# State space input weights from tables of powers spread in DRAM instead of 64 transposes, with two additions held back and another order of the last stores

## The chip, the cores and the metric

The kernel runs on one core of one Trainium2 chip. Its engines are TensorE (PE in the profile, with its weight loads as PEld), VectorE (DVE), ScalarE (ACT), GpSimd (POOL) and SyncE (SP, which here only issues DMAs). The metric is the device time in microseconds; the time of a kernel is the median of its runs. One execution is also recorded by the profiler. All durations below come from that execution, and its span runs from the first to the last instruction.

## The reference, cut to what matters

A one-layer encoder over two sequences of 512 tokens with 1024 channels: three branches (a state space branch, differential attention, cross attention to a memory), gated and summed, then a gated feed-forward part and a final RMS norm. All of it is f32. The change touches the state space branch and the end:

```python
lam_bar = jnp.exp(lam * step[:, None])
b_bar = ((lam_bar - 1.0) / lam)[..., None] * b
bu = jnp.einsum('lgh,gph->lgp', u.astype(jnp.complex64), b_bar)
_, xs = lax.associative_scan(_ssm_combine, (a, bu), axis=0)
...
return x + (jax.nn.silu(gate) * up) @ p['w_ffn_out'][l]
...
return _rmsnorm(x, p['norm_final'])
```

There are 32 groups (g) of 16 channels (h) and 64 complex states, in two directions, so that 2 x 64 states fill the 128 partitions.

## The kernel before, in words

Every large product is made on TensorE from a high and a low part of each f32 operand (three products `xh*wh`, `xl*wh`, `xh*wl`, each 128x128 by 512 columns). `weight` (L146) loads a 128x1024 tile of weights by an SP DMA into `wf` (two buffers); `split` casts it to `wh` on ScalarE (L134) and subtracts to get `wl` on VectorE (L135), two buffers each. The order of work is: memory projections (`mem_k`, `mem_v`), norm of the inputs x (`x_norm`, L252 to L254), four tiles of the u projection (weights `w_in[0]` to `w_in[3]`), gate projections with the state space work in between, gelu and its gate product, cross attention, differential attention, merge, output product, feed-forward, final norm.

The state space branch is a generator, `s5_gen`, advanced by `next(s5)` at fixed places of the program:

- the second step, during `mem_k`, computes powers 0 to 8 of `lam_bar` (`pr`, `pi`) and the factor `gr`, `gi` on VectorE in small operations (L1433 to L1544);
- the third, issued on SP behind the load of `w_in[1]`, loads `b` and `c` (L1549 to L1552);
- the fourth, behind the split of `w_in[1]` on ScalarE and VectorE, makes `b_r`, `b_i` (b times the factor), copies the powers turned for the two directions (`qr`, `qi`, `xr_`, `xi_`, L1564 to L1567) and calls `input_weights` for three of the four blocks of eight groups;
- the fifth, after the u projection in the program, makes `output_weights` 0 and 1, loads `u_`, multiplies it by the input weights (L1668), makes the fourth block of input weights and `output_weights` 2 and 3;
- then the scan over 64 chunks of 8 tokens (four VectorE operations each, L1683 to L1686), and the outputs (L1727 to L1729).

`input_weights(o)` multiplies, on VectorE, `b_r` and `b_i` by the powers (six operations of 128x1024, L1590 to L1592). The result has the states on the partitions; the product with u needs (token in chunk, channel) there. So each of its 16 blocks of 128x128 is transposed on TensorE (L1604) into PSUM and copied out by ScalarE (L1605): 64 transposes and 16 copies of 512 columns in all.

Near the end, the feed-forward output product runs in 12 visits of 128 output rows by a seven-product scheme. In the last eight of its 36 pieces the weights' sums are not prepared ahead: `raw_sums` (L452 to L455) makes four of them on GpSimd, ScalarE (L137) and VectorE (L138) split them, and TensorE uses them one piece later. At the end of each visit GpSimd adds four quadrants to y (L1301), in the order c11, c22, c21, c12.

The final norm goes in three column ranges (512, 256, 256). In the last one TensorE spreads the row factors into PSUM (L69), ScalarE copies them to SBUF for GpSimd (L1356), GpSimd scales rows 0 to 2 (L1359) and VectorE rows 3 to 7 (L1364), and SP stores pairs of rows (L1367).

The order of instructions on each engine is set when the kernel is built: a planner takes the ready instruction that stands first in the program, by a simulated timeline; some blocks are told to come after a given instruction of the same engine (`queued()`: after the last weight load on SP; `yielding(...)`: after a split). At run time each engine, and SP's queue, goes in that fixed order and waits where it must.

Of the kernel before, what the change touches and what calls it, by code (L numbers as in the profile page):

```python
# [10 lines left out]
F32 = mybir.dt.float32  # L11
# [61 lines left out]
def encoder(ctx: ExitStack, tc: tile.TileContext, a, out):  # L73
# [375 lines left out]
    def raw_sums(raw):  # L449

        a21, a11, a12, a22 = (raw[:, i] for i in range(4))
        PO.tensor_tensor(out=a22, in0=a21, in1=a22, op=ALU.add)  # L452
        PO.tensor_tensor(out=a21, in0=a11, in1=a21, op=ALU.subtract)
        PO.tensor_tensor(out=a11, in0=a22, in1=a11, op=ALU.subtract)
        PO.tensor_tensor(out=a12, in0=a12, in1=a11, op=ALU.subtract)  # L455
# [770 lines left out]
    n_w, last_7, last_h = 0, None, None  # L1226

    def w_room(n):
        nonlocal n_w
# [3 lines left out]

    def weights7(i, m, p, n):

        nonlocal last_w, last_7, last_h
# [29 lines left out]
    next(coming[0], None)  # L1266
    with queued(), tc.issue_after(last_h.ins):
        nxt = act_pair(2, third=V)
    n_p = 0
    for v, (m, lo_, hi_) in enumerate(VISITS):  # L1270
        ps = [bank() for _ in range(6)] + [aux()]
        for p in range(lo_, hi_):
            if n_p + 3 < len(pieces) and not pieces[n_p + 3][2]:
                next(coming[n_p + 3])
            if n_p + 2 < len(pieces):
                next(coming[n_p + 2])
            for g in coming[n_p + 1 : n_p + 2]:
                for _ in g:
                    pass
            th, tl = pairs[p]  # L1280
            w = made[n_p]
            n_p += 1
            if v < 4 and p == 1:
                with queued():
                    for t in (m, m + 4):
                        nc.sync.dma_start(y[t], x1D[t])
            for p_, (nm, o) in zip(ps, SEVEN):
                wh, wl = w[nm]
                PE.matmul(p_, wh, th[:, o], start=(p == lo_), stop=False)
                PE.matmul(p_, wh, tl[:, o], start=False, stop=False)  # L1290
                PE.matmul(p_, wl, th[:, o], start=False, stop=(p == hi_ - 1))
            if v == 3 and p == 0:
                with queued(), tc.issue_after(last_sum.ins):
                    pair_in()
            if (v, p) in ((10, 7), (10, 8), (11, 7), (11, 8)):
                keep(2)
        ps = iter(ps)
        c11, c12, c21, c22 = quadrants(ps, next(ps), ("nsq", "nsq"))
        for c_, t, s in ((c11, 0, 0), (c22, 4, 1), (c21, 4, 0), (c12, 0, 1)):
            yv = y[m + t][:, s * L : (s + 1) * L]  # L1300
            PO.tensor_tensor(out=yv, in0=yv, in1=c_, op=ALU.add)  # L1301
        if v == 0:
            with tc.issue_after(last_sum.ins):
                pairs.append(quad_split(2, *nxt))
            with tc.issue_after(last_q[1].ins):
                activate(1, gf1, up1)
        elif v == 1:
            with queued(), tc.issue_after(last_sum.ins):
                pair_in()
        if v == 2:  # L1310
            with queued():
                nc.sync.dma_start(aD[KFF - 1], ac)
        if v == 7:
# [36 lines left out]
    def final(ss, c0, n, ready=(), late=()):  # L1350

        cs = slice(c0, c0 + n)
        _, bc = factor(ss, DM, n // P)
        if ready:
            b_ = new_acc()
            S.copy(b_[:, :n], bc[:, :n])  # L1356
        for m in (0, 1, 4, 5, 6, 7, 2, 3) if late else range(KD):
            if m in ready:
                PO.tensor_tensor(out=y[m][:, cs], in0=y[m][:, cs], in1=b_[:, :n], op=ALU.mult)  # L1359
            else:  # L1360
                with ExitStack() as es_:
                    if m in late:
                        es_.enter_context(tc.issue_after(last_add.ins))
                    V.scalar_tensor_tensor(out=y[m][:, cs], in0=y[m][:, cs], scalar=vcol("norm_final", m), in1=bc[:, :n],  # L1364
                                           op0=ALU.mult, op1=ALU.mult)
            if m % 2 == 1:
                nc.sync.dma_start(out[c0 // L, :, m - 1 : m + 1, c0 % L : c0 % L + n], y2[m // 2][:, :, cs])  # L1367
            yield

# [79 lines left out]
def s5_gen(k):  # L1449
# [67 lines left out]
    def cmul(eng, outr, outi, ar, ai, br, bi, t1, t2):  # L1517
# [4 lines left out]
        eng.tensor_tensor(out=t2, in0=ai, in1=br, op=ALU.mult)  # L1522
        eng.tensor_tensor(out=outi, in0=t1, in1=t2, op=ALU.add)

    ta, tb = (pp.tile([P, 512], F32, name=n_) for n_ in ("ta", "tb"))
# [26 lines left out]
    nc.sync.dma_start(cn, a["c_im"])  # L1552
    yield

    V.tensor_scalar_mul(cn, cn, -1.0)
    b_r, b_i = cp.tile([P, G, 16], F32, name="b_r"), cp.tile([P, G, 16], F32, name="b_i")
    bs = [P, G, 16]
    cmul(V, b_r, b_i, br, bi, gr.unsqueeze(2).broadcast_to(bs), gi.unsqueeze(2).broadcast_to(bs),
         ta.rearrange("p (g h) -> p g h", h=16), tb.rearrange("p (g h) -> p g h", h=16))

    qr, qi = cp.tile([P, 8, G], F32, name="qr"), cp.tile([P, 8, G], F32, name="qi")
    xr_, xi_ = cp.tile([P, 8, G], F32, name="xr_"), cp.tile([P, 8, G], F32, name="xi_")
    for (q_, x_, s_) in ((qr, xr_, pr), (qi, xi_, pi)):
        S.copy(q_[0:64], s_[0:64, 7::-1, :])  # L1564
        S.copy(q_[64:128], s_[64:128, 0:8, :])
# [27 lines left out]
        return tiles  # L1593


    def input_weights(o):
        res = []
        for w_ in cprod("it", by_group(b_r, o), by_group(b_i, o), by_token(qr, o), by_token(qi, o), True):
            w_ = w_.rearrange("p g e h -> p (g e h)")
            t_ = slot("wb", [P, 8 * P], name="wb")  # L1600
            for g4 in range(2):
                tr = aux()
                for g in range(4):
                    PE.transpose(tr[:, g * P : (g + 1) * P], w_[:, (4 * g4 + g) * P : (4 * g4 + g + 1) * P], ident)  # L1604
# [57 lines left out]
    for o in range(4):  # L1662
        for ri, w_ in enumerate(wbs[o]):
            for g4 in range(2):
# [110 lines left out]
def layout(i):  # L1775
# [31 lines left out]
    a["log_step"] = dpg(np.broadcast_to(i["s5_log_step"][0][:, :, None], (2, G, 64)))  # L1807
    for nm in ("re", "im"):
        b = i["s5_b_" + nm][0]
        a["b_" + nm] = b.transpose(0, 2, 1, 3).reshape(P, G, 16)  # L1810
        c = i["s5_c_" + nm][0]
        a["c_" + nm] = c.transpose(0, 3, 1, 2).reshape(P, G, 16)
# [21 lines left out]
```

## Time and profile before

| | |
|---|---|
| median of 3 runs | 1589.17 us (1587.68 to 1589.8) |
| the profiled execution | 1588.24 us |
| its span | 1586.5 us |
| mean granted TensorE clock | 0.998 |
| instructions | 21339 |
| TensorE instructions | 7736 matmuls and as many weight loads |
| HBM read, written | 165.16 MB, 71.27 MB |

A row of a group of instructions names line, engine, operation, what is written from what, and the shape; then the count, the busy time and the mean of one. Matmuls overlap in the pipeline, so the start of one to the start of the next is what one costs, and not its duration. In a row of the timeline the first number is the start in us and the second how long the (merged) entry took; idle time before it, and what ended it, stands in brackets.

### The profile page before, as it was taken

To read this page: it belongs to the slowest core of one execution; us is meant where nothing else is said; L and a number is where in the kernel's file an instruction comes from. 1 tells how busy PE (TensorE), PEld (TensorE's weight loads), DVE (VectorE), ACT (ScalarE), POOL (GpSimd) and SP (SyncE) were. 2 spreads that over 40 slices of the span, in tenths; PEclk is the share of its full clock that TensorE was granted. 3 is DMA by queue.
4 is the path that set the end of the run, shared out by engine and by line. 5 is a ranking of instruction groups with operands and counts; after the bars stand their busy time and mean duration, and the time that the engine had idled before them with its cause. 6 is when DMAs were issued, how large, how long until landed. Compare 5 with 4: busy or idle time off the path is not lost. (4 is left out here: it accounts for less than half of the span.)

```text
span 1586.5 us, 21339 instructions
## 1 busy us (share of the span) xinstructions
PE 1573.4 (99%) x7736; PEld 1311.3 (83%) x7736; DVE 1169.2 (74%) x1859; ACT 631.9 (40%) x1115; POOL 550.7 (35%) x434
## 2 busy tenths in 40 slices
PE   9999999999999999999999999999999999999997
PEld 7888888888898779778888888888888888888777
DVE  7978995076774776866545669888888877888864
ACT  7644223265553365563223443333333324222323
POOL 0010000001333320300443355777777553444763
PEclk9999999999999999999999999999999999999999
DMA  9554623676762121135544422323333323885412
GB/s 359 186 170 127 204 94 119 179 266 205 266 223 107 41 100 41 47 127 179 196 143 126 141 86 93 119 101 120 120 128 125 114 85 124 319 315 189 152 56 107
DMA packets 105610, 237.84 MB, mean 150 GB/s; under 512 B 13600, under 2 KB 45344, under 8 KB 105504
## 3 DMA queue, kind: packets, MB, share of 16 engines
q1 hardware_dynamic: 105360, 236.45, 44.4%
q8 instruction: 61, 1.00, 0.3%
q14 instruction: 45, 0.37, 0.1%
q10 hardware_dynamic: 144, 0.02, 0.0%
HBM read 165.16 MB, written 71.27 MB: 149 GB/s over the span
## 5 line engine op out<-in xcount | busy, mean ns | idle before, releaser
L66 PE MATMUL bkmm<-xh,wh 128*128 128x512 f32 x640 | 255.6, 399 | 0.0
L66 PE MATMUL bkmm<-xh,wl 128*128 128x512 f32 x640 | 250.9, 392 | 0.0
L66 PE MATMUL bkmm<-xl,wh 128*128 128x512 f32 x640 | 250.4, 391 | 0.0
L66 PE MATMUL bkmm<-tl,wh 128*128 128x512 f32 (+1 forms) x621 | 241.4, 389 | 0.0
L66 PE MATMUL bkmm<-th,wl 128*128 128x512 f32 (+1 forms) x621 | 241.0, 389 | 0.0
L66 PE MATMUL bkmm<-th,wh 128*128 128x512 f32 (+1 forms) x621 | 240.9, 389 | 0.0
L134 ACT CAST wh<-wf 128x1024 fp32r<-128x1024 f32 (+2 forms) x134 | 117.6, 878 | 265.4 <-PE bkmm L66 190.7
L135 DVE TENSOR_TENSOR wl<-wf,wh 128x1024 fp32r<-128x1024 f32 (+2 forms) x134 | 147.6, 1102 | 61.0 <-ACT wh L134 45.7
L66 PE MATMUL bkmm<-th,w 128*128 128x512 f32 x432 | 140.6, 392 | 2.6 <-ACT w L137 2.1
L66 PEld LDWEIGHTS bkmm<-xh,wh 128*128 128x128 f32 x640 | 120.4, 188 | 26.2 <-issue 3.4
L66 PEld LDWEIGHTS bkmm<-xh,wl 128*128 128x128 f32 x640 | 120.3, 188 | 26.0 <-issue 0.4
L66 PEld LDWEIGHTS bkmm<-xl,wh 128*128 128x128 f32 x640 | 120.5, 188 | 22.3
L66 PEld LDWEIGHTS bkmm<-th,wl 128*128 128x128 f32 x621 | 116.6, 188 | 24.0
L66 PEld LDWEIGHTS bkmm<-th,wh 128*128 128x128 f32 x621 | 116.6, 188 | 23.9
L66 PEld LDWEIGHTS bkmm<-tl,wh 128*128 128x128 f32 x621 | 116.7, 188 | 23.8
L1175 POOL TENSOR_TENSOR up<-up,acc 128x512 f32<-128x512 f32 x44 | 83.7, 1919 | 90.7 <-DVE up L1112 87.0
L452 POOL TENSOR_TENSOR raw<-raw 128x128 f32<-128x128 f32 x28 | 14.7, 523 | 287.4 <-DVE nb L543 230.7
L66 PEld LDWEIGHTS bkmm<-th,w 128*128 128x128 f32 x432 | 81.0, 188 | 22.0 <-ACT w L137 3.0
L792 POOL TENSOR_TENSOR mg<-mg,gl 128x1024 f32<-128x1024 f32 x16 | 43.8, 2740 | 136.8 <-DVE gl L788 132.1
L66 PE MATMUL bkmm<-tl,w 128*128 128x512 f32 x216 | 84.2, 390 | 0.0
L134 ACT CAST wh<-ws 128x1024 fp32r<-128x1024 f32 x44 | 46.3, 1053 | 91.5 <-PE bkmm L66 49.8
L66 PE MATMUL bkmm<-yh,wh 128*128 128x512 f32 x192 | 76.3, 397 | 0.0
(661 smaller groups left out, 3534.6 us busy)
## 6 DMA issues: line engine op xcount, KB each, us to landing
wf<-in_w_in SPq DMA_DIRECT2D x40, 512.0 KB, 3.9
wD<-hl SPq DMA_DIRECT2D x28, 512.0 KB, 2.9
w<-wD SPq DMA_DIRECT2D x28, 512.0 KB, 5.2
gD<-gt SPq DMA_DIRECT2D x24, 512.0 KB, 2.8
gl<-gD SPq DMA_DIRECT2D x24, 512.0 KB, 3.7
wf<-in_w_fg SPq DMA_DIRECT2D x22, 512.0 KB, 3.6
wf<-in_w_fu SPq DMA_DIRECT2D x22, 512.0 KB, 3.5
aD<-ac SPq DMA_DIRECT2D x22, 512.0 KB, 2.8
```

What stands on the lines that cost most here:

```text
L66: return self.put(self.eng.matmul(*args, **kw))
L134: h = S.copy(hi, src)
L135: l_ = V.tensor_tensor(out=lo, in0=src, in1=hi.bitcast(F32), op=ALU.subtract)
L452: PO.tensor_tensor(out=a22, in0=a21, in1=a22, op=ALU.add)
L792: PO.tensor_tensor(out=mg[m], in0=mg[m], in1=gt, op=ALU.add)
L1175: PO.tensor_tensor(out=up, in0=up, in1=accs[s], op=ALU.mult)
```

## The change

1. **Input weights in turned layout.** The powers times the factor (`qgr`, `qgi`) are made once for all groups (six VectorE operations of 256 columns) in the second step, with the copies of the powers moved there. In the third step TensorE transposes them (4 transposes, one ScalarE copy), four DMAs store them to DRAM (`qD`, 64 KB each), and eight DMAs copy them inside DRAM to `qR`, 16 times each (512 KB each, 4 MB in all). For each block two tables of 512 KB are loaded from `qR` and two of b, already turned by the host and repeated for the 8 tokens, from a new input. `input_weights` is then six VectorE operations on plain 128x1024 tiles, and no transposes and copies.
2. **Order.** `output_weights` 0 and 1 and their stores move into the fourth step, in front of input weights 0 to 2. The fourth block is made after the second block of states instead of the first; its tables take slots of tags `it` and `wb`.
3. **Additions.** In visits 8 and 9 the addition of c12 is held back, to the second piece of the next visit, behind the last `raw_sums` on GpSimd.
4. **End.** In the last range the factors are spread twice, into two PSUM tiles: VectorE reads one, ScalarE copies the other. Each row has its own store; those of rows 0 to 2 are issued by ScalarE.

```diff
-        PO.tensor_tensor(out=a12, in0=a12, in1=a11, op=ALU.subtract)
+        return PO.tensor_tensor(out=a12, in0=a12, in1=a11, op=ALU.subtract)
...
-            raw_sums(raw)
+            last_r = raw_sums(raw)
...
+            if p == lo_ + 1:
+                with ExitStack() as es_:
+                    if held:
+                        es_.enter_context(tc.issue_after(last_r.ins))
+                    for yv, c_ in held:
+                        PO.tensor_tensor(out=yv, in0=yv, in1=c_, op=ALU.add)
+                held = []
...
-            PO.tensor_tensor(out=yv, in0=yv, in1=c_, op=ALU.add)
+            if v in (8, 9) and c_ is c12:
+                held.append((yv, c_))
+            else:
+                PO.tensor_tensor(out=yv, in0=yv, in1=c_, op=ALU.add)
...
-        _, bc = factor(ss, DM, n // P)
+        rs, bc = factor(ss, DM, n // P)
         if ready:
             b_ = new_acc()
-            S.copy(b_[:, :n], bc[:, :n])
+            if c0 > L:
+                b2 = aux()
+                for t in range(n // P):
+                    PE.transpose(b2[:, t * P : (t + 1) * P], rs[:, t : t + 1].broadcast_to([P, P]), ident)
+                S.copy(b_[:, :n], b2[:, :n])
+            else:
+                S.copy(b_[:, :n], bc[:, :n])
...
-            if m % 2 == 1:
+            if c0 > L:
+                q = nc.scalar if m in ready else nc.sync
+                q.dma_start(out[c0 // L, :, m, c0 % L : c0 % L + n], y[m][:, cs])
+            elif m % 2 == 1:
...
+    qr, qi = (t_[:, 8 * G :].rearrange("p (e g) -> p e g", g=G) for t_ in (ta, tb))
+    for (q_, s_) in ((qr, pr), (qi, pi)):
+        S.copy(q_[0:64], s_[0:64, 7::-1, :])
+        S.copy(q_[64:128], s_[64:128, 0:8, :])
+    cmul(V, qgr, qgi, qr, qi, gr.unsqueeze(1).broadcast_to(qs_), gi.unsqueeze(1).broadcast_to(qs_), t84a, t84b)
     yield
+    for ri, q_ in enumerate((qgr, qgi)):
+        for hf in range(2):
+            PE.transpose(tr[:, (2 * ri + hf) * P : (2 * ri + hf + 1) * P],
+                         q_[:, 4 * hf : 4 * hf + 4, :].rearrange("p e g -> p (e g)"), ident)
+    S.copy(qt.rearrange("p a n -> p (a n)"), tr)
+    for ri in range(2):
+        for hf in range(2):
+            nc.sync.dma_start(qD[ri, 4 * hf : 4 * hf + 4].rearrange("e g n -> (e g) n"), qt[:, 2 * ri + hf])
+    qR = drp.tile([2, 4, 8, 16, 8 * P], F32, name="qR")
+    for o in range(4):
+        for ri in range(2):
+            nc.sync.dma_start(qR[ri, o], qD[ri, :, 8 * o : 8 * o + 8].rearrange("e g n -> e (g n)").unsqueeze(1).broadcast_to([8, 16, 8 * P]))
...
+    def tables_in(o, qtag, tag):
+        for ri, nm in enumerate(("bt_re", "bt_im")):
+            q_ = slot(qtag, [P, 8 * P], name="qT")
+            nc.sync.dma_start(q_, qR[ri, o].rearrange("e h n -> (e h) n"))
+            b_ = slot(tag, [P, 8 * P], name="bT")
+            nc.sync.dma_start(b_, a[nm][:, 8 * P * o : 8 * P * (o + 1)])
+            tabs += [q_, b_]
...
-        for w_ in cprod("it", by_group(b_r, o), by_group(b_i, o), by_token(qr, o), by_token(qi, o), True):
+        for x1, x2, op in ((bt_r, bt_i, ALU.subtract), (bt_i, bt_r, ALU.add)):
             t_ = slot("wb", [P, 8 * P], name="wb")
-            for g4 in range(2):
-                tr = aux()
-                for g in range(4):
-                    PE.transpose(tr[:, g * P : (g + 1) * P], w_[:, (4 * g4 + g) * P : (4 * g4 + g + 1) * P], ident)
-                S.copy(t_[:, g4 * 512 : g4 * 512 + 512], tr)
+            t1 = slot("it", [P, 8 * P], name="ct1")
+            V.tensor_tensor(out=t1, in0=x1, in1=q_r, op=ALU.mult)
+            V.tensor_tensor(out=t_, in0=x2, in1=q_i, op=ALU.mult)
+            V.tensor_tensor(out=t_, in0=t1, in1=t_, op=op)
...
-    wbs = [input_weights(o) for o in range(3)]
-    yield
+    tab0 = tables_in(0, "mem", "mem")
...
     output_weights(0)
     output_weights(1)
+    wbs = [input_weights(o, *t_) for o, t_ in enumerate(((), ("it", "mem"), ("mem", "mem")))]
+    yield
...
-        if o == 0:
-            wbs.append(input_weights(3))
+        if o == 1:
+            wbs.append(input_weights(3, "it", "wb"))
```

More of the change, by code (lines that the diff above doesn't have):

```diff
@@ L1224, in keep @@
             kept.append((k0[:, i - 1], k1[:, i - 1], raw[:, i % 2]) if i else raw[:, 0])
-    n_w, last_7, last_h = 0, None, None
+    n_w, last_7, last_h, last_r = 0, None, None, None
     def w_room(n):
@@ L1234, in weights7 @@
     def weights7(i, m, p, n):
-        nonlocal last_w, last_7, last_h
+        nonlocal last_w, last_7, last_h, last_r
         raw = None
@@ L1268, in encoder @@
         nxt = act_pair(2, third=V)
-    n_p = 0
+    n_p, held = 0, []
     for v, (m, lo_, hi_) in enumerate(VISITS):
@@ L1523, in cmul @@
         eng.tensor_tensor(out=outi, in0=t1, in1=t2, op=ALU.add)
+    qgr, qgi = pp.tile([P, 8, G], F32, name="qgr"), pp.tile([P, 8, G], F32, name="qgi")
     ta, tb = (pp.tile([P, 512], F32, name=n_) for n_ in ("ta", "tb"))
@@ L1544, in s5_gen @@
     V.tensor_tensor(out=gi, in0=gi, in1=dn, op=ALU.mult)
-    yield
+    qr, qi = (t_[:, 8 * G :].rearrange("p (e g) -> p e g", g=G) for t_ in (ta, tb))
+    for (q_, s_) in ((qr, pr), (qi, pi)):
+        S.copy(q_[0:64], s_[0:64, 7::-1, :])
+        S.copy(q_[64:128], s_[64:128, 0:8, :])
+    qs_ = [P, 8, G]
+    cmul(V, qgr, qgi, qr, qi, gr.unsqueeze(1).broadcast_to(qs_), gi.unsqueeze(1).broadcast_to(qs_), t84a, t84b)
+    yield
+    qD = drp.tile([2, 8, G, P], F32, name="qD")
+    tr = aux()
+    for ri, q_ in enumerate((qgr, qgi)):
+        for hf in range(2):
+            PE.transpose(tr[:, (2 * ri + hf) * P : (2 * ri + hf + 1) * P],
+                         q_[:, 4 * hf : 4 * hf + 4, :].rearrange("p e g -> p (e g)"), ident)
+    qt = ta.rearrange("p (a n) -> p a n", n=P)
+    S.copy(qt.rearrange("p a n -> p (a n)"), tr)
[6 more added lines that the diff above has]
+            nc.sync.dma_start(qR[ri, o], qD[ri, :, 8 * o : 8 * o + 8].rearrange("e g n -> e (g n)").unsqueeze(1).broadcast_to([8, 16, 8 * P]))
     br, bi = pp.tile([P, G, 16], F32, name="br"), pp.tile([P, G, 16], F32, name="bi")
@@ L1553, in s5_gen @@
     yield
[L1555 to L1561, printed above, removed]
     xr_, xi_ = cp.tile([P, 8, G], F32, name="xr_"), cp.tile([P, 8, G], F32, name="xi_")
-    for (q_, x_, s_) in ((qr, xr_, pr), (qi, xi_, pi)):
-        S.copy(q_[0:64], s_[0:64, 7::-1, :])
-        S.copy(q_[64:128], s_[64:128, 0:8, :])
+    for (x_, s_) in ((xr_, pr), (xi_, pi)):
         S.copy(x_[0:64], s_[0:64, 1:9, :])
@@ L1593, in cprod, with input_weights @@
         return tiles
-    def input_weights(o):
+    def tables_in(o, qtag, tag):
+        gs = slice(8 * o, 8 * o + 8)
+        tabs = []
+        for ri, nm in enumerate(("bt_re", "bt_im")):
[4 more added lines that the diff above has]
+            tabs += [q_, b_]
+        return tabs
+    def input_weights(o, *tags):
+        q_r, bt_r, q_i, bt_i = tables_in(o, *tags) if tags else tab0
         res = []
-        for w_ in cprod("it", by_group(b_r, o), by_group(b_i, o), by_token(qr, o), by_token(qi, o), True):
-            w_ = w_.rearrange("p g e h -> p (g e h)")
+        for x1, x2, op in ((bt_r, bt_i, ALU.subtract), (bt_i, bt_r, ALU.add)):
             t_ = slot("wb", [P, 8 * P], name="wb")
-            for g4 in range(2):
-                tr = aux()
-                for g in range(4):
-                    PE.transpose(tr[:, g * P : (g + 1) * P], w_[:, (4 * g4 + g) * P : (4 * g4 + g + 1) * P], ident)
-                S.copy(t_[:, g4 * 512 : g4 * 512 + 512], tr)
+            t1 = slot("it", [P, 8 * P], name="ct1")
+            V.tensor_tensor(out=t1, in0=x1, in1=q_r, op=ALU.mult)
+            V.tensor_tensor(out=t_, in0=x2, in1=q_i, op=ALU.mult)
+            V.tensor_tensor(out=t_, in0=t1, in1=t_, op=op)
             res.append(t_)
         return res
-    wbs = [input_weights(o) for o in range(3)]
-    yield
+    tab0 = tables_in(0, "mem", "mem")
+    V.tensor_scalar_mul(cn, cn, -1.0)
+    b_r, b_i = cp.tile([P, G, 16], F32, name="b_r"), cp.tile([P, G, 16], F32, name="b_i")
+    bs = [P, G, 16]
+    cmul(V, b_r, b_i, br, bi, gr.unsqueeze(2).broadcast_to(bs), gi.unsqueeze(2).broadcast_to(bs),
+         ta.rearrange("p (g h) -> p g h", h=16), tb.rearrange("p (g h) -> p g h", h=16))
     gD = drp.tile([G, 16, 15, 16], F32, name="gD5")
@@ L1809, in layout @@
         b = i["s5_b_" + nm][0]
+        bt = b.transpose(3, 1, 0, 2).reshape(1, 16, G * P)
+        a["bt_" + nm] = np.broadcast_to(bt, (8, 16, G * P)).reshape(P, G * P)
         a["b_" + nm] = b.transpose(0, 2, 1, 3).reshape(P, G, 16)
```

## The prediction

> **What bounds the kernel now.** I read the page first. Its head, the busy times and the DMA line:
>
> ```profile
> span 1586.5 us, 21339 instructions
> ...
> PE 1573.4 (99%) x7736; PEld 1311.3 (83%) x7736; DVE 1169.2 (74%) x1859; ACT 631.9 (40%) x1115; POOL 550.7 (35%) x434
> ...
> DMA  9554623676762121135544422323333323885412
> ```
>
> TensorE is busy for all but 13 us, so the time is TensorE's issue time plus the few places where it stands. The waits of TensorE by releaser name the largest of these, two stalls of 2.1 us together behind a ScalarE split:
>
> ```profile
> PE bkmm L66 <- ACT w L137: 2.1, 2, 1.1
> ```
>
> Work taken off TensorE, or a stall ended, is therefore worth its full time, as long as nothing else makes TensorE wait. The groups of TensorE, then its timeline around the first block of transposes (start, then duration of the merged entry):
>
> ```profile
> L1604 PE MATMUL bktr<-ident,cxr 128*128 128x128 f32 x32 | 4.3, 272 | 0.0
> L1604 PE MATMUL bktr<-ident,cxi 128*128 128x128 f32 x32 | 4.1, 273 | 0.0
> ```
>
> ```profile
> 71.65 0.39 PE L66 MATMUL bkmm<-xh,wh 128*128 128x512 f32 x1
> ...
> 73.92 0.40 PE L66 MATMUL bkmm<-xl,wh 128*128 128x512 f32 x1
> 74.15 1.04 PE L1604 MATMUL bktr<-ident,cxr 128*128 128x128 f32 x8
> 74.94 0.48 PE L66 MATMUL bkmm<-xh,wl 128*128 128x512 f32 x1
> 75.26 0.39 PE L66 MATMUL bkmm<-xh,wh 128*128 128x512 f32 x1
> ```
>
> The reader is to see that durations overlap: ten matmuls start within 73.92 - 71.65 = 2.27 us, so one costs 0.227 us, not 0.39.
>
> **The transposes.** From 73.92 to 75.26 are 1.34 us; two matmul steps would take 0.45. The other 0.89 us are eight transposes: 0.111 us each. 64 go (7.1 us), four for the tables of powers come (0.4): **-6.7 us**.
>
> The Trainium skill (TensorE: Matmul & The Clock Gate, Part 4: PE-mode transpose) gives about 275 ns for a transpose in a kernel's context; at that 60 fewer would save 16.5 us. The trace has 272 ns as the duration, but starts 0.111 us apart, and the starts decide.
>
> **The additions.** GpSimd, ScalarE and TensorE at the first of the two stalls, one timeline each:
>
> ```profile
> 1491.90 1.44 POOL L452 TENSOR_TENSOR acc<-acc 128x128 f32<-128x128 f32 x1
> 1493.30 2.27 POOL L1301 TENSOR_TENSOR y<-y,nsq 128x512 f32<-128x512 f32 x1
> ```
>
> ```profile
> 1497.71 0.63 ACT L137 ACTIVATE w<-acc 128x512 fp32r<-128x512 f32 x1 [5.89 <-POOL acc L455]
> ```
>
> ```profile
> 1496.99 0.39 PE L66 MATMUL bkmm<-th,w 128*128 128x512 f32 x1
> 1498.39 0.50 PE L66 MATMUL bkmm<-th,w 128*128 128x512 f32 x1 [1.02 <-ACT w L137]
> 1498.73 0.40 PE L66 MATMUL bkmm<-tl,w 128*128 128x512 f32 x1
> 1499.23 0.74 PE L66 MATMUL bkmm<-th,w 128*128 128x512 f32 x2
> ```
>
> The addition of c12 stands between the sums L452 and L453 of the piece that TensorE needs next. Held back, it lets the sums end about 2.2 us sooner. The stall is 1.40 - 0.23 = 1.17 us, and 0.50 - 0.23 = 0.27 one step later, 1.44 in all, under 2.2; the second is alike: **-2.9 us**. The held addition waits on GpSimd behind the sums of the piece after; behind it stands nothing that is due before the next visit's end, and y is read only in the last range. If the sums came in another order, 0 of this would remain.
>
> **The end.** The timeline of all engines at the end, and SP's row for the stores:
>
> ```profile
> 1579.62 0.37 ACT L1356 COPY acc<-bktr 128x256 f32<-128x256 f32 x1 [0.89 <-PE bktr L69]
> 1580.03 2.05 DVE L1364 SCALAR_TENSOR_TENSOR y<-y,vec,bktr 128x256 f32<-128x256 f32 x5 [1.10 <-ACT acc L1356]
> 1580.07 2.08 POOL L1359 TENSOR_TENSOR y<-y,acc 128x256 f32<-128x256 f32 x3 [1.39 <-ACT acc L1356]
> ```
>
> ```profile
> L1367 SPq DMA_DIRECT2D out_y<-y x12: 372/372/457, 1561.6 to 1582.8; - x12
> ```
>
> VectorE starts only when ScalarE has copied the factors; with its own PSUM tile it may start up to 0.4 us sooner. GpSimd's three rows then end last, at 1582.15, later by the two added transposes, 0.2 us. Their store goes out on ScalarE at once, while now SP issues its last one at 1582.8. That is 1582.8 - 1582.35: **-0.4 us** (bounds: -0.8 if both sides gain, +0.3 if ScalarE's issue is slower than SP's).
>
> **What the tables cost before the u projection.** VectorE, then TensorE:
>
> ```profile
> 47.83 3.38 DVE L252 SCALAR_TENSOR_TENSOR xt<-xt,vec,bktr 128x512 f32<-128x512 f32 x5 [0.43 <-PE bktr L69]
> ...
> 52.33 1.22 DVE L135 TENSOR_TENSOR wl<-wf,wh 128x1024 fp32r<-128x1024 f32 x1
> ...
> 58.72 0.69 DVE L1518 TENSOR_TENSOR ta<-br,gr 128x512 f32<-128x512 f32 x1
> ```
>
> ```profile
> 53.64 0.48 PE L66 MATMUL bkmm<-xh,wl 128*128 128x512 f32 x1
> ```
>
> VectorE has no gap here but 0.43 us. The six new products of 256 columns stand before this in the program, and so in the planner's order: 0.35 us each (half of 0.69), at most 0.69, hence 2.1 to 4.1 us. The low part `wl` of w_in[0] is ready at 53.55 and used at 53.64; there is no cover. 2.1 - 0.43 - 0.1: **+1.6 us**, bounds 0 (planned behind `wl`) and 3.6. I take the low price of the product, since duration goes nearly with width in this view.
>
> **What the copies in DRAM cost.** SP's timeline, the DMA issues from 60 to 100 us, one stretch with full DMA queues, and ScalarE's casts from 38 to 82 us:
>
> ```profile
> 53.58 0.34 SPq L146 DMA_DIRECT2D wf<-in_w_in x1
> ...
> 59.33 0.38 SPq L146 DMA_DIRECT2D wf<-in_w_in x1
> ```
>
> ```profile
> uD<-ut SPq DMA_DIRECT2D x3, 512.0 KB, 2.8
> ```
>
> ```profile
> 20.00:40.00 20.00, 20.00 (x91) 16.46 (x90) 17.93 (x86) 14.45 (x26) 0.00 (x0) 1.00 1.03 405
> ```
>
> ```profile
> L134 ACT CAST wh<-wf x6: 1044/1052/1058, 38.2 to 76.0; 128x1024 fp32r<-128x1024 f32 x6
> ```
>
> No copy from DRAM to DRAM is in this trace. Eight of 0.524 MB are 4.19 MB: 10.4 us at the 405 GB/s of the full stretch, 20.7 us if each byte counts twice, as read and as write. I take 20.7, since a copy loads the same memory on both sides. The powers' products end near 45 us, transposes, copy and store follow, and the store lands by about 52 us. The copies then start ahead of the load of w_in[2] (53.58). It comes in at 52 + 20.7 + 1.3 (its own 0.524 MB) + 1.5 (2.8 less 1.3, to landing) = 75.5 us, and is cast at 76.5. TensorE wants it after the 96 matmuls of w_in[0] and w_in[1]: 53.2 + 1.6 + 21.8 = 76.6 us. With the loads of b and c in the same queue (1.05 MB, 2.6 us) it is 2.5 us late, without them on time: **+1.0 us**, bounds 0 and (below) 20.
>
> **At nothing.** The products of the input weights stay 24 of 128x1024, and plain ones are no dearer than spread ones (1.22 us for `wl` above). ScalarE loses 16 copies. The table loads, 16 of 0.524 MB or 21 us at 405 GB/s, lie in slices 2 to 4 of the DMA line, half of which are free (some 60 of 119 us); were the cover gone, a late weight would cost TensorE up to the 10.9 us that a tile lasts (48 matmuls). The states may come some us earlier or later:
>
> ```profile
> 254.15 2.37 DVE L1720 COPY x<-st 64x2048 f32<-64x2048 f32 x2
> ```
>
> ```profile
> L1728 PE MATMUL bktr<-x,c_r x64: 274/275/276, 269.4 to 312.1; 128*128 128x128 f32 x64
> ```
>
> The scan's result is copied by 256.5 and first used at 269.4: 12.9 us of cover.
>
> **Sum.** -6.7 - 2.9 - 0.4 + 1.6 + 1.0 = **-7.4 us**: 1588.24 for the profiled execution becomes 1580.8. The median is 0.93 above it: 1589.17 - 7.4 = **1581.8 us**. The bounds of the terms give it a range of its own from 1578.7 to 1584.5.
>
> **Rivals.**
> - *No new wait* (0.20): the planner puts the products behind `wl` and the copies are over in time. -10.0 us: 1579.2. For it speaks that the 64 old transposes waited on VectorE too and TensorE never stood there; against it the 0.1 us of cover.
> - *The gain goes into SP's queue* (0.18): the table loads wait for slots that VectorE frees and for the copies to land, and SP goes in order, so that a gate's weight behind them is late by 4 to 8 us. Only the end's and the additions' 3.3 us are sure: 1585.9 to 1589.9, about 1588. For it: three more kinds of waits in one queue. Against it: two `wf` buffers, each good for 10.9 us.
> - *Slower* (0.24): the copies run on half of the DMA engines and each at half rate: 41.4 us. w_in[2], and w_in[3], which is issued 5.7 us later, come in behind them: 52 + 41.4 + 1.3 + 1.5 + 1.05 = 97.2 us against 76.6, a stall of 20.6 us. -8.4 + 20.6 = +12.2: 1601.4. It decides from copies of 20.7 + 8.4 = 29 us on. For it: the first of the copy's dimensions is 8, not 128. Against it: nothing in this trace shows a store or a load on part of the engines. The Trainium skill (DMA: Bandwidth & Descriptors, Why a DMA increments its semaphore by 16 and not by 1) has it that the number of engines is the largest up to 16 that divides the slowest dimension on both sides, so 8 here; by it alone, at 20.7 us on all engines, this rival would come true. No row here tests it.
>
> **How the numbers follow.** The forecast has 0.38. About 0.2%, 3.2 us, is what a measurement of this kernel can tell from no change. Faster: 0.38 + 0.20 and 0.08 of the second rival, 0.66; same: its other 0.10; slower: 0.24. The range goes from 1578.2 (0.04 below) to 1597.0, which takes in copies of up to 37 us and leaves out some 0.13 of the third rival.
>
> **What would show it.** Right: 60 fewer L69/L1604 transposes and a shorter busy time of TensorE by 6 to 7 us; no stall behind ACT w L137 after visits 8 and 9; last store issued before 1582.4 less the gain. A stall of 1 to 2 us at the first matmul with `wl` of the u projection, and one of up to 2.5 us at w_in[2], would show the two added terms. Wrong: a TensorE wait of over 8 us between 75 and 100 us, behind a cast whose load landed late; then the copies' time is the failed step. Waits spread over 100 to 260 us would point to SP's queue, and a late scan (after 267 us) to the states.

## The result and the profile after

The changed kernel takes **1608.53 us** (median of 4 runs, 1607.7 to 1609.31) against 1588.82 us for the kernel before (4 runs on the same chip). The ratio is 1.0124, with a 95% interval of 1.0112 to 1.0137: slower by 19.7 us, where 7.4 us less was forecast. The profiled execution took 1608.71 us. Its page begins:

```profile
span 1606.9 us, 21266 instructions
...
PE 1575.6 (98%) x7678; PEld 1310.3 (82%) x7678; DVE 1171.9 (73%) x1865; ACT 622.0 (39%) x1100; POOL 549.3 (34%) x434
...
DMA  9677442667664120125553432333333323786412
```

TensorE has 58 matmuls fewer (64 transposes go, 4 and 2 come), but is not busy for less: 1575.6 us against 1573.4. Its waits by releaser have new names:

```profile
PE bktr L1684 <- DVE cxi L1624: 7.6, 1, 7.6
PE bkmm L66 <- DVE wl L135: 3.6, 3, 1.6
PE bktr L1717 <- issue: 3.6, 1, 3.6
PE bktr L1717 <- DMA u__1164<-uD: 2.8, 1, 2.8
PE bkmm L66 <- DVE nsq L1112: 1.2, 2, 0.6
```

**Where the time was lost.** Apart from the transposes TensorE does the same matmuls in both kernels, so the starts of one group tell how far it lags. The groups of the first products with the scan's result, and of the last weights of the feed-forward product, for the changed kernel (the first of these rows stands in the prediction for the kernel before, from 269.4):

```profile
L1777 PE MATMUL bktr<-x,c_r x64: 274/275/276, 290.9 to 333.6; 128*128 128x128 f32 x64
```

```profile
L66 PE MATMUL bkmm<-th,wh x621: 278/389/482, 952.9 to 1585.7; 128*128 128x512 f32 x154, 128*128 128x256 f32 x2
```

and the second for the kernel before:

```profile
L66 PE MATMUL bkmm<-th,wh x621: 278/389/483, 931.3 to 1564.3; 128*128 128x512 f32 x154, 128*128 128x256 f32 x2
```

The lag is 290.9 - 269.4 = 21.5 us at the state space outputs, 21.6 at the first feed-forward output weight, 21.4 at the last, and 20.4 at the end of the span. So all of the loss is made ahead of the state space outputs. TensorE there, in the changed kernel:

```profile
56.28 0.50 PE L66 MATMUL bkmm<-xh,wh 128*128 128x512 f32 x1 [0.92 <-ACT wh L134]
...
56.85 0.39 PE L66 MATMUL bkmm<-xh,wl 128*128 128x512 f32 x1
...
96.36 0.39 PE L66 MATMUL bkmm<-xh,wh 128*128 128x512 f32 x1
104.40 0.72 PE L1684 MATMUL bktr<-cxi,l 128*48 128x144 f32 x4 [7.64 <-DVE cxi L1624]
...
119.65 5.44 PE L1717 MATMUL bktr<-u__1164,wb 128*128 128x128 f32 x32 [2.77 <-DMA u__1164<-uD]
...
149.31 6.61 PE L1717 MATMUL bktr<-u__1164,wb 128*128 128x128 f32 x32 [3.56 <-issue]
```

The first product with `wl` of the u projection starts at 56.85, 3.2 us later than before (53.64). From there to the outputs the lag grows by 18.3 us although 64 transposes go, 7.1 us (the four new ones stand ahead of 56.85), so 25.4 us are lost. The rows give most of it: 7.8 us at 104.40 (8.04 from start to start, less one step), 2.9 and 3.7 us at the states (L1717), about 4 us at the three waits for `wl`, which come at 234 to 258 us, in the scan. Most of the rest is the clock. The windows that hold the three long stalls (the third number from the end is the granted clock):

```profile
104.00:108.00 4.00, 3.60 (x33) 3.40 (x33) 3.90 (x4) 0.92 (x3) 0.00 (x0) 0.57 0.40 74
119.00:125.00 6.00, 5.35 (x33) 5.38 (x34) 0.00 (x0) 0.00 (x0) 0.00 (x0) 0.72 0.83 282
149.00:156.00 7.00, 6.68 (x34) 6.68 (x35) 5.06 (x7) 2.44 (x6) 0.00 (x0) 0.56 1.00 368
```

After each stall TensorE is granted a lower clock for some us (0.50 in the stretch from 104.4 to 107.2): 4.0 x 0.43 + 6.0 x 0.28 + 7.0 x 0.44 = 6.5 us, of which some 0.4 fall on time in which it stood. 7.8 + 2.9 + 3.7 + 4 + 6.1 is 24.5 of the 25.4.

**What is behind the 7.6 us.** SP's queue in the changed kernel (start, how long the entry held the queue), then VectorE:

```profile
61.07 2.08 SPq L1583 DMA_DIRECT2D qD<-ta  x4
63.25 0.38 SPq L146 DMA_DIRECT2D wf<-in_w_in  x1
63.73 10.80 SPq L1587 DMA_DIRECT2D qR<-qD  x8
74.65 2.20 SPq L1633 DMA_DIRECT2D qT<-qR  x1
...
80.22 1.28 SPq L1635 DMA_DIRECT2D bT<-in_bt_im  x1
...
92.00 0.33 SPq L146 DMA_DIRECT2D wf<-in_w_in  x1
```

```profile
48.92 1.22 DVE L135 TENSOR_TENSOR wl<-wf,wh 128x1024 fp32r<-128x1024 f32 x1
...
95.78 2.36 DVE L1646 TENSOR_TENSOR wb<-bT,qT 128x1024 f32<-128x1024 f32 x2 [15.74 <-DMA bT<-in_bt_im]
...
103.03 1.23 DVE L1624 TENSOR_TENSOR cxi<-ct,cxi 128x1024 f32<-128x1024 f32 x1
...
125.45 1.23 DVE L1645 TENSOR_TENSOR ct<-bT,qT 128x1024 f32<-128x1024 f32 x1 [9.86 <-DMA gD<-gk]
...
132.05 2.36 DVE L1646 TENSOR_TENSOR wb<-bT,qT 128x1024 f32<-128x1024 f32 x2 [5.37 <-DMA qT<-qR]
```

The powers' store goes out at 61.07, the copies hold SP from 63.73 to 74.53, and the first block's last table is in only at 95.8. VectorE goes in order: it has planned that block's products ahead of the rest of `output_weights(1)`, stands 15.74 us, and makes `cxi` by 104.26, for which TensorE has waited since 96.6. It stands again at 125 and 132, so states and scan come late. (The releaser named at 125.45 is a store of `gD`, which this product doesn't read; whether a table or a free slot was waited for there is open.) In the scan VectorE is busy for 30.7 of the 32 us from 230 to 262, and the weights' `wl` come 12.6 to 13.2 us apart, where TensorE needs one every 10.9 us.

### The profile page after: what moved, and what is told of

It is laid out like the page before. It is cut to its first block, busy times and chain, and to the rows that moved or that the text cites. A ratio compares the mean times of both kernels' runs of the same rounds, so it can differ in the third digit from the quotient of the medians.

```text
span 1606.9 us, 21266 instructions
## 1 busy us (share of the span) xinstructions
PE 1575.6 (98%) x7678; PEld 1310.3 (82%) x7678; DVE 1171.9 (73%) x1865; ACT 622.0 (39%) x1100; POOL 549.3 (34%) x434
## 5 line engine op out<-in xcount | busy, mean ns | idle before, releaser
L135 DVE TENSOR_TENSOR wl<-wf,wh 128x1024 fp32r<-128x1024 f32 (+2 forms) x134 | 152.7, 1140 | 50.1 <-ACT wh L134 45.7
L66 PEld LDWEIGHTS bkmm<-xl,wh 128*128 128x128 f32 x640 | 120.5, 188 | 22.7 <-issue 0.6
```

The lines of the kernel that those rows point to most:

```text
L66: return self.put(self.eng.matmul(*args, **kw))
L135: l_ = V.tensor_tensor(out=lo, in0=src, in1=hi.bitcast(F32), op=ALU.subtract)
```

## The experiments

My theory after the first look was that the copies and the tables' way through DRAM make the loss; rivals were the tail's parts, and the new order. Times of the kernel before lie at 1588.66 to 1588.84 us in all groups; the ratio is to it.

**The tail's parts.** `b_tail` is the kernel before with the held additions and the new end, `a_notail` the changed kernel without them.

```diff
+            if v in (8, 9) and c_ is c12:
+                held.append((yv, c_))
...
+                PE.transpose(b2[:, t * P : (t + 1) * P], rs[:, t : t + 1].broadcast_to([P, P]), ident)
+                S.copy(b_[:, :n], b2[:, :n])
```

> The kernel before with the held additions and the new end alone. If the tables of powers are the whole loss (theory 1): the last column range ends 1.0 us sooner, as in the profile of the changed kernel, and the additions give 0 to 1.4 us, so 1.0 to 2.4 us faster than before. If the tail itself costs (rival): slower than before by 1 us or more. The prediction had 3.3 us faster.

> The changed kernel without the held additions and the new end, so turned input weights alone. Theory 1: 1609 to 1611 us, 1 to 2.4 us slower than the changed kernel, with the same stalls of TensorE between 95 and 260 us. Rival (the tail costs): 1600 us or less.

`b_tail` took 1587.39 us (ratio 0.9993, 0.9984 to 1.0002), `a_notail` 1610.02 (1.0135, 1.0121 to 1.0149). The two parts give some 1.4 us either way (for `b_tail` alone the interval still holds 1) and are no cause of the loss. TensorE's stalls in `b_tail`, and VectorE at the first:

```profile
1506.05 0.50 PE L66 MATMUL bkmm<-th,w 128*128 128x512 f32 x1 [0.61 <-DVE nsq L1112]
1514.03 0.74 PE L66 MATMUL bkmm<-th,w 128*128 128x512 f32 x2 [0.41 <-DVE w L138]
1522.37 0.51 PE L66 MATMUL bkmm<-th,w 128*128 128x512 f32 x1 [0.60 <-DVE nsq L1112]
```

```profile
1504.34 1.05 DVE L138 SCALAR_TENSOR_TENSOR w<-acc,w 128x512 fp32r<-128x512 f32 x1
1505.32 0.68 DVE L1112 TENSOR_TENSOR nsq<-bkmm,u 128x512 f32<-128x512 f32 x1
```

The two stalls behind ScalarE at 1498 and 1514 are gone, but three smaller ones have come: in two of them a split on VectorE goes just ahead of the quadrant's sum that empties the PSUM bank which TensorE wants.

**The copies.** `a_host` is the changed kernel without the copies; where a table of powers was loaded it loads b's table from the host once more, so the powers are left out of the result and no load waits for them. The four stores stay. `a_16` turns the copies' slowest dimension from 8 to 16.

```diff
-            nc.sync.dma_start(q_, qR[ri, o].rearrange("e h n -> (e h) n"))
+            nc.sync.dma_start(q_, a[nm][:, 8 * P * o : 8 * P * (o + 1)])
```

```diff
-            nc.sync.dma_start(qR[ri, o], qD[...].unsqueeze(1).broadcast_to([8, 16, 8 * P]))
+            nc.sync.dma_start(qR[ri, o].rearrange("e h n -> h e n"), qD[...].unsqueeze(0).broadcast_to([16, 8, 8 * P]))
```

> The changed kernel without the copies inside DRAM: the tables of powers are replaced by loads of the input b again, so the input weights are b times b instead of b times powers, and nothing waits for the powers; same number and size of table loads, same place of output weights. Theory 1 (the copies and what waits for them make the stalls): the stalls of 7.6 and 2.8 us at 104 and 120 us go, and those of 3.6 us at 149 and of 3.6 us in all at 234 to 258 us with them, and the lower clock after them: 1580 to 1588 us. Rival (the moved output weights and the late fourth block make the scan late, whatever the tables wait for): 1600 us or more, the stalls at 234 to 258 us stay.

> The changed kernel with the dimensions of the copies in another order, 16 outermost instead of 8, same bytes and same result. Theory 1 with copies on 8 of 16 engines: with 16 engines busy the 4.19 MB pass in 10 to 12 us instead of 20, the tables land about 10 us sooner, the 7.6 us stall goes and the whole is 8 to 15 us faster than the changed kernel: 1594 to 1600 us. If the number of engines is not what holds the copies: 8 engines busy as before and within 2 us of 1608.5. Rival (order of the work): also within 3 us of 1608.5, even if the copies get faster.

`a_host` took 1595.16 us (1.0037, 1.0023 to 1.005), `a_16` 1600.33 (1.0074, 1.006 to 1.0088). Without the copies, and with tables that wait for no powers, 13.4 us of the loss go; 6.3 stay. Its profiled execution took 1592.85 us, 2.3 less than the median, and TensorE still stands in it, for 4.1 us in three waits at the states and 2.4 us in two for `wl`. With copies on all engines 8.2 us go. In `a_16` the stall of 7.6 us behind `cxi` is gone, and the later ones stand as they did:

```profile
PE bkmm L66 <- DVE wl L135: 3.7, 3, 1.6
PE bktr L1717 <- issue: 3.5, 1, 3.5
PE bktr L1717 <- DMA u__1164<-uD: 3.4, 1, 3.4
```

So that stall, with the slower clock after it, is about what the slow copies cost. The window in which the copies run, in the changed kernel and in `a_16` (the last two numbers are the DMA engines' busy share and GB/s):

```profile
66.00:78.00 12.00, 12.00 (x55) 9.89 (x53) 10.07 (x12) 3.96 (x10) 4.77 (x1) 1.00 0.53 185
```

```profile
70.00:78.00 8.00, 8.00 (x41) 6.40 (x41) 5.69 (x7) 3.74 (x8) 3.48 (x1) 1.00 1.00 372
```

Half of the engines are busy, and they move half as much: 185 GB/s on 0.53 of them, 372 on all (in `b_copies`, next, 162 GB/s on 0.48 from 55 to 66 us). Each busy engine thus moves as much in both, and the copies run on half of them. The Trainium skill's rule (DMA: Bandwidth & Descriptors, Why a DMA increments its semaphore by 16 and not by 1), by which the slowest dimension of 8 gives 8 engines and one of 16 all of them, agrees with both traces (0.53 and 1.00 busy).

`b_copies` puts stores and copies alone into the kernel before; nobody reads them. `b_copies2` puts the loads of b and c ahead of them.

```diff
+    nc.sync.dma_start(qD[ri, 4 * hf : 4 * hf + 4]..., (pr, pi)[ri][:, 4 * hf : 4 * hf + 4, :]...)
+    nc.sync.dma_start(qR[ri, o], qD[ri, :, 8 * o : 8 * o + 8]...unsqueeze(1).broadcast_to([8, 16, 8 * P]))
     nc.sync.dma_start(br, a["b_re"])
```

> The kernel before, with the four stores and the eight copies inside DRAM alone added (of the plain powers; nobody reads the copies, transposes and order are as before). They stand in SP's queue ahead of the load of w_in[2], as the prediction had them. If copies run on half of the engines, at full rate on each (20 us for 4 MB): w_in[2] up to 5 us late, 1590 to 1595. If on half of the engines and at half rate: 41 us, 1600 to 1612. If the copies cost nothing by themselves and the loss of the changed kernel comes from VectorE's wait for the tables: 1588 to 1590.

> The kernel before with the stores and the copies inside DRAM (read by nobody), where the loads of b and c stand ahead of them in SP's queue; with those loads behind them it took 1598.0 us, and TensorE stood 7.7 us behind VectorE, which waited 11.6 us for the load of c_im. If that one load was the price, the wait is gone: 1588.5 to 1590.5, also if the next weight is some us late, since w_in[3] has two buffers ahead of it. If the copies themselves take the DMA engines from everything behind them, another wait takes its place (w_in[3] or the stores of the u projection): 1593 to 1598.

`b_copies` took 1598.04 us (1.0057, 1.0043 to 1.0072), `b_copies2` 1591.94 (1.0021, 1.0012 to 1.003). In `b_copies`, SP, VectorE and TensorE:

```profile
54.00 6.23 SPq L1554 DMA_DIRECT2D qR<-qD  x8
60.27 6.06 SPq L1560 DMA_DIRECT2D cn<-in_c_im  x1
```

```profile
80.95 0.43 DVE L1563 TENSOR_SCALAR cn<-cn 128x512 f32<-128x512 f32 x1 [11.58 <-DMA cn<-in_c_im]
```

```profile
83.92 1.94 PE L1612 MATMUL bktr<-ident,cxi 128*128 128x128 f32 x8 [7.71 <-DVE cxi L1600]
```

Read the four rows as one chain. One load of 256 KB stands behind the copies, holds SP for 6.06 us and lands at 80.9. VectorE, in order, stands 11.58 us for a 0.43 us negation that nobody wants yet, and TensorE stands 7.71 us for what is planned behind it. In `b_copies2`, where the loads of b and c and w_in[2] go ahead of the copies, this stall is gone and 6.1 us come back. So 4 MB of copies that nobody reads cost 3.3 us beside this kernel's other loads, and 9.2 us in the other order of the queue, most of it through this one load. w_in[2], which the prediction watched, is not what TensorE waited for in `b_copies`, though it stood behind all eight copies.

**The order.** `a_hostord` is `a_host`, and `a_16ord` is `a_16`, each with output weights 0 and 1 behind the input weights again.

```diff
-    output_weights(0)
-    output_weights(1)
     wbs = [input_weights(o, *t_) for o, t_ in ...]
     yield
+    output_weights(0)
+    output_weights(1)
```

> The changed kernel with its tables of powers read from a host input (no store, no copies inside DRAM; the powers are left out of the result) took 1595.2 us against 1588.7 before. Here, besides, output weights 0 and 1 go back behind the input weights, as before the change. If the new order makes the rest of the loss (VectorE's products of the input weights and output weights in an order in which each waits for the other's partner, states and scan 11 us late): 1584 to 1588, scan again at about 150 us, waits of TensorE for wl at 209 to 258 us gone. If the tables themselves make it (loads that wait for free slots, VectorE behind them): 1593 to 1597, scan again at about 159 us.

> The changed kernel with the copies' slowest dimension 16 instead of 8 took 1600.3 us, 8.2 less than the changed kernel, copies on 16 engines. Here, besides, output weights 0 and 1 go back behind the input weights. If the order costs by itself, the two gains add: 1592 to 1596. If the tables' way (store, copies, loads, VectorE in order behind them) is what holds the states, the old order only moves TensorE's wait from the output weights to the states: 1598 to 1602, and the wait at 110 us goes up.

`a_hostord` took 1588.29 us (0.9999, 0.9989 to 1.0008), 6.9 less than `a_host`; `a_16ord` 1604.33 (1.0095, 1.0081 to 1.011), 4.0 more than `a_16`. So the new order has no fixed price. Where tables are early it costs, where they come through DRAM it pays. It gives VectorE other work while the tables are on their way: from 50 to 170 us VectorE is busy for 85.1 us in `a_16` and for 70.0 in `a_16ord`. And even without any copy, in the old order, the turned layout gains nothing, though 8.4 us less was forecast without the copies. In `a_hostord` TensorE still stands at the first products and at the states (its profiled execution took 1590.51 us, 2.2 more than the median):

```profile
55.66 0.50 PE L66 MATMUL bkmm<-xh,wh 128*128 128x512 f32 x1 [0.49 <-ACT mf L368]
57.72 0.69 PE L66 MATMUL bkmm<-xh,wl 128*128 128x512 f32 x1 [1.33 <-DVE wl L135]
```

```profile
PE bktr L1713 <- DVE st L1717: 1.6, 2, 1.1
```

**Only some blocks.** These are built on `b_tail`, in the old order, without copies: each table is spread from the small store by eight DMAs of 16 partitions. `c_o2` has block 2 alone in turned layout, `c_o12` and `c_o23` two blocks; `c_l2`, `c_l12` and `c_l123` make the powers' products and the store later, behind input weights 0; `a_directord` is the changed kernel in the old order with such loads in place of the copies, so it has all four blocks.

```diff
+            for e in range(8):
+                nc.sync.dma_start(q_[16 * e : 16 * e + 16], qD[ri, e, 8 * o : 8 * o + 8]...unsqueeze(0).broadcast_to([16, 8 * P]))
...
-    wbs = [input_weights(o) for o in range(3)]
+    wbs = [input_weights(0), input_weights(1), turned(2, "mem", "mem")]
```

> The kernel before, with the tail's parts of the change, and with the turned layout for the third block alone, in the old order, its tables spread from the small store straight into the tiles (16 DMAs of 16 partitions, no copies inside DRAM). Sixteen transposes and four ScalarE copies go (1.7 us less TensorE work), four transposes come. If it is the copies and the tables' slots for all blocks that cost the change its gain: 1584.5 to 1587, no wait of TensorE over 1 us between 75 and 150 us. If any table load in SP's queue costs as much as its transposes: 1588 to 1591.

> Blocks 1 and 2 in turned layout, tables straight from the small store, old order, tail's parts, powers' products and the store early (second and third step, store at about 61 us). Against the run with the same blocks and the late store (1597.8). If lateness of the tables is the price: VectorE's wait for the first table falls from 16.3 us to under 4, since the first table lands at about 74 us where the product stands at 74 to 78, and the time is 1584.5 to 1588.5. If the layout itself costs (loads of 16 partitions that hold SP's queue and the engines' rings): 1593 to 1598 again.

> Blocks 2 and 3 in turned layout, tables straight from the small store, old order, tail's parts, early store. The run with block 2 alone took 1587.6 with no wait for a table. If a block whose tables are in time gains its transposes (16 times 0.111 us, 1.8 us): 1585 to 1586.5. If the fourth block's tables wait for slots that VectorE and TensorE free only at 120 to 130 us: states and scan late, waits of TensorE for wl at 200 to 260 us, 1588 to 1593.

> Block 2 alone in turned layout with the powers' products behind the first block's in the fourth step, so that the store stands behind other work in SP's queue. With the early store it took 1587.6 and TensorE stood 1.07 us at 56 us. If lateness is the price and block 2 is late enough in the order: the 1.07 us go and nothing comes, 1586 to 1587; if the late store (about 83 us, tables landing at 94 and later) is behind VectorE's place for the block (about 90 us): 1588 to 1593, with VectorE's wait for a table in place of TensorE's at 56 us.

> The kernel before with the tail's parts, blocks 1 and 2 in turned layout by loads straight from the small store, in the old order, and the powers' products in the fourth step, behind input weights 0. Against the kernel with the tail's parts alone (1587.4): 32 transposes go and 4 come, 28 times 0.111 us or 3.1 us. If the products in the second step were what ate the gain with one block (a wait of 1.07 us at 56 us): 1583.5 to 1585.5. If tables of any kind make the states late: 1587 to 1590, with waits of TensorE at 100 to 160 us.

> As the kernel with blocks 1 and 2 turned, and block 3 as well, with its tables in slots that the input weights use otherwise. Against the tail's parts alone (1587.4): 48 transposes go and 4 come, 44 times 0.111 us or 4.9 us: 1581.5 to 1584 if the loads stay hidden. If the slots of the fourth block's tables come free too late, the scan starts late and TensorE waits for wl at 200 to 260 us: 1585 to 1590.

> The changed kernel with the whole computation, but without the copies inside DRAM: each table of powers is loaded from the small store by eight DMAs, each of which spreads one row over 16 partitions; and output weights 0 and 1 stand behind the input weights again. If the copies and the order they forced made the loss (VectorE in order behind the tables), it is near the kernel with host tables in the old order (1588.3), plus what block 0 waits for the store: 1588 to 1592. If any way through DRAM is too late for block 0 (powers at 54 us, store at 61, load at 66 and later, where the kernel before has its first block at 65 to 70): 1592 to 1600, with VectorE's longest wait at the first table.

| kernel | us | ratio (95%) | first use of the scan at |
|---|---|---|---|
| b_tail (no block) | 1587.39 | 0.9993 (0.9984 to 1.0002) | 269.5 |
| c_o2 | 1587.63 | 0.9993 (0.9984 to 1.0002) | 270.1 |
| c_o23 | 1592.02 | 1.0020 (1.0011 to 1.0029) | 272.5 |
| c_l2 | 1593.77 | 1.0028 (1.0016 to 1.0039) | 277.0 |
| c_o12 | 1594.51 | 1.0038 (1.0026 to 1.0051) | 277.3 |
| c_l12 | 1597.84 | 1.0052 (1.0039 to 1.0064) | 278.1 |
| c_l123 | 1604.90 | 1.0106 (1.0092 to 1.0120) | 284.1 |
| a_directord | 1610.63 | 1.0136 (1.0122 to 1.0150) | 289.5 |

The last column is the start of the first product with the scan's result, and the total follows it. My expectations for `c_l12`, `c_l123`, `c_o12` and `a_directord` were too hopeful: leaving out the copies isn't enough. In `a_directord` TensorE stands 13.6 us for one `cxi`, and VectorE 13.2 us in three waits for `qT`. (Of the runs above, `a_host`, `b_copies` and `b_copies2` came out between the times named for the two sides, and `a_16ord` above both.) What counts in the traces is when the tables come. `c_l2` differs from `c_o2` in the place of the products and the store; VectorE in it:

```profile
DVE ct L1658 <- DMA qT<-qD: 10.4, 1, 10.4
```

In `c_o2` the block's tables were in before VectorE came to them, and it had no such wait. TensorE's stall there is an earlier one, at the u projection:

```profile
56.07 0.50 PE L66 MATMUL bkmm<-xh,wh 128*128 128x512 f32 x1 [1.07 <-ACT wh L134]
```

In `c_l12` the store is issued at 82.91 only, behind loads of `u_`, and VectorE stands 16.34 us:

```profile
82.91 1.82 SPq L1642 DMA_DIRECT2D qD<-ta  x4
```

```profile
93.78 1.22 DVE L1658 TENSOR_TENSOR ct<-bT,qT 128x1024 f32<-128x1024 f32 x1 [16.34 <-DMA qT<-qD]
```

In `c_o12` the store is early, but the second block's tables stand among the `u_` loads in SP's queue, and VectorE stands until they are through; the releaser named is `u_`, whose loads stand around the table's in that queue:

```profile
89.40 1.23 DVE L1658 TENSOR_TENSOR ct<-bT,qT 128x1024 f32<-128x1024 f32 x1 [5.74 <-DMA u__1201<-uD]
...
96.26 1.23 DVE L1659 TENSOR_TENSOR wb<-bT,qT 128x1024 f32<-128x1024 f32 x1 [4.49 <-DMA u__1201<-uD]
```

So in each of these VectorE stands for tables that are late, and late tables, not the layout by itself, are the price: `c_l2` and `c_o2` have the same loads, and the late store costs 6.1 us. But not every late table comes from a late store. In `c_o12` the eight loads of one table hold SP for 4 to 5 us (4.86, 4.13, 4.36 and 4.70), and its 1594.5 us lie in the range that its expectation gives to the price of such loads. How much of them is the loads' own price is not shown. Only block 2 was tried alone, and it costs nothing; its 12 fewer transposes (1.3 us) are about what the stall of 1.07 us at 56 us takes, which `b_tail` doesn't have. No version was measurably faster than the kernel before; `b_tail` and `c_o2` come closest.

## Why the prediction was wrong, point by point

- **The transposes, -6.7: taken as right, not seen alone.** The count fits. The marker, a busy time of TensorE 6 to 7 us shorter, failed: it is 2.2 us longer, and matmuls at the lower clock, which last longer, make up most of the difference (6.1 us by the windows).
- **At nothing: the step that failed.** It held the four tables of each block to be covered by free DMA time, and looked only at a weight behind them. It left out who reads them: VectorE, in order, with `output_weights` and the weights' `wl` behind. VectorE stood 15.74 us for the first block's last table, and TensorE 7.64 us for the `cxi` behind it. With table loads but no way through DRAM (`a_host`) there is a loss of 6.3 us, where 8.4 us less was due without the copies; in the old order (`a_hostord`) there is none, but none of the 8.4 either; with the way through DRAM it is 19.7. The cover of 12.9 us for late states shrank to 5.5 us, but held: the scan starts 32.7 us later (180.9 against 148.2), x is copied by 285.4 and first used at 290.9. What the late scan cost TensorE are the waits for `wl` in it. (In `a_16ord` the cover did run out: TensorE stands 7.1 us for x.)
- **The copies in DRAM, +1.0: failed too.** They begin at 63.7 and not at 52: the products end at 53.8, not 45, and ScalarE copies the four transposes only at 60.5, behind other copies. So w_in[2] is ahead of them, as nothing in the prediction had it. The 20.7 us of copying were about right (4.19 MB at the window's 185 GB/s are 22.7 us, an estimate), but they come from half of the engines, as the third rival had it, and not from bytes that count twice (`b_copies` moves 4.46 MB more than the kernel before, stores and copies once each); "each at half rate" was wrong. The way through DRAM, copies and the wait for the powers together, costs 13.4 us in this order, through the tables; copies on all engines alone give 8.2 back.
- **The products before the u projection, +1.6:** 3.2 us later at the first `wl`, of which 0.6 was there at 27 us, before any product: 2.6, within the bounds. The way was another: VectorE's later `wl` (48.92, before 46.18) frees a `wf` buffer later, and the next weight's load and cast follow (the 0.92 us behind `wh` at 56.28).

```profile
46.18 1.23 DVE L135 TENSOR_TENSOR wl<-wf,wh 128x1024 fp32r<-128x1024 f32 x1
```

- **The additions, -2.9: mis-sized.** In `b_tail` the lag goes from +0.1 to -0.4 over the feed-forward product, in the changed kernel from 21.6 to 21.4: 0.5 and 0.2 us. In `a_notail`, without them, it falls from 21.9 to 21.6 as well, so hardly any of it is theirs for certain. The stalls behind ScalarE went, but the sum left out VectorE, whose order puts new ones in their place.
- **The end, -0.4: 1.0** (lag 21.4 at the last weight, 20.4 at the end; in `a_notail` it falls by 0.2). VectorE starts as soon as TensorE has spread the factors, and three stores go out on ScalarE:

```profile
1600.97 2.05 DVE L1380 SCALAR_TENSOR_TENSOR y<-y,vec,bktr 128x256 f32<-128x256 f32 x5 [0.59 <-PE bktr L69]
...
1602.39 1.70 ACTq L1384 DMA_DIRECT2D out_y<-y  x3
```

- **The rivals.** "The gain goes into SP's queue" named the mechanism (loads that wait for slots and copies, waits over 100 to 260 us), but let only a weight be late and so stopped at no gain. Two of the prediction's own signs came with it, waits spread over 100 to 260 us and a scan used after 267 us. "Slower" named half of the engines rightly, but its stall behind w_in[2] didn't come, so that its 12.2 us slower has the right sign by luck. The Trainium skill's rule on the slowest dimension was set aside with "No row here tests it" and a chance of 0.24 for this rival; the rule held.

What stays open: the old order takes back the 6.3 us that `a_host` loses, and of the 8.4 us that were due besides some 2.5 are the additions' and 1.0 the products'. Where the others went, to slots, to SP's queue or to the planner's order, can't be told apart further, since each edit moved the order of all engines.

## What to carry to other kernels

When work goes from a compute engine to tables in DRAM, follow the table to its reader: list what stands behind the reading instruction on its in-order engine, and set the time at which the last table lands (producer, copy, store, copy, load, each behind its own queue) against the time at which that engine comes to it. Free DMA time is no cover for a chain of copy, store, copy and load. And a wait removed by moving one instruction should be sought again on the other engines of the same chain before its full price is written down.

## What the runs showed of the hardware

- The queue that issues DMAs can be held up itself while earlier transfers are on their way: the eight copies held SP for 10.80 us in the changed kernel and 6.54 in `a_16`. In `b_copies` they held it for 6.23 us, and the one load behind them for 6.06 us, where loads of that size took 0.43 to 0.49 us ahead of the copies.
- After the stalls of 7.6, 2.8 and 3.6 us the granted clock fell for some us (windows above), which added about 6.1 us to 14 us of stalls. In `a_hostord` it fell after one of 1.33 us (0.79 from 55 to 63 us); after those of 1.02 and 1.10 us near the end of the kernel before it stayed at full (1.00 from 1496 to 1502 and from 1512 to 1520 us).
